# A low-rank-adapted matrix product: W on the sync queue, other load pieces, warm-up transpositions, no early store

## The chip, the cores and the metric

The kernel runs on one core of a Trainium2 chip. The metric is the device time of one execution in microseconds (us); lower is better. The profiled span, from the first to the last instruction of the program, is about 1.3 us shorter than that time.

## The reference

```python
x: (16, 2048, 256) float32      # 32768 rows of 256
W: (256, 256); lora_A: (256, 16); lora_B: (16, 256); lora_E: (16,); scale = 1.0

y = x_flat @ W
lora_out = ((x_flat @ lora_A) * lora_E) @ lora_B
return (y + scale * lora_out).reshape(16, 2048, 256)
```

x is 33.6 MB and y is 33.6 MB, and each has to cross between HBM and the on-chip memory once. The kernel folds the low-rank part into the weight, `weff = W + scale * A·diag(E)·B`, and does one product of x with `weff` in bf16.

## The kernel before

x is cut into eight chunks of 4 MB (128 partitions, 32 rows of 256 floats in each). Six "homes" hold a chunk each; the result overwrites x in its home, and chunks 6 and 7 take the homes of chunks 0 and 1 once these have been stored. Every chunk is worked on in eight groups of four rows. A group goes from POOL (cast to bf16) to PE (transposition), ACT (copy out of PSUM, the memory that PE writes to), PE (product) and DVE (copy back into the home). The sync engine issues all the x loads and y stores; their order is a list. All small operands come through the scalar engine's queue.

```python
LOAD_PIECES = {0: [8, 8, 16]}          # chunk 0 is loaded in three pieces
ORDER = ["L0", "L1", "L2", "L3", "L4", "L5",
         "S0", "S1", "L6", "L7", "S2", "S3", "S4", "S5", "S6", "S7"]
EARLY_AFTER = 1
...
def load(pc):                          # sync engine
    c, s, e = pc
    if c == N_HOMES - 1:
        sync.wait_ge(s_weff, 1)        # W, A, B lie in the last home until weff is made
    if c >= N_HOMES:
        sync.wait_ge(stored_of[c - N_HOMES], 16)
    ...
for step in ORDER:
    if step[0] == "L":
        ...load the pieces of chunk c...
        if c == EARLY_AFTER:           # the early store: 16 partitions x 128 B of group 0
            sync.wait_ge(s_first, 1)   # DVE has finished group 0
            sync.dma_start(out=y_chunks[0, :16, 0, :32], in_=home(0)[:16, 0, :32]).then_inc(s_early, 16)
    else:
        sync.wait_ge(s_chunk, c + 1)
        if c == 0:
            sync.wait_ge(s_early, 16)
        sync.dma_start(out=y_chunks[c], in_=home(c)[:])...
...
# PE, after the set-up products and turn(0), turn(1):
for i in ...:                          # software pipeline, PE works in this order
    turn(i + 2)                        # four transpositions of group i + 2
    multiply(i)                        # eight products of group i
```

Of the kernel before, what the change touches and what calls it, by code (L numbers as in the profile page):

```python
# [7 lines left out]
P = 128  # L8
# [5 lines left out]
ROWS = 32  # L14
N_CHUNKS = 8
N_HOMES = 6
LOAD_PIECES = {0: [8, 8, 16]}

ORDER = [
    "L0", "L1", "L2", "L3", "L4", "L5",  # L20
    "S0", "S1", "L6", "L7", "S2", "S3", "S4", "S5", "S6", "S7",
]

EARLY_AFTER = 1

HELD = N_HOMES - 1

CG = 4
# [9 lines left out]
def kernel(  # L38
# [16 lines left out]
    KT = K // P  # L55
# [3 lines left out]
    y_chunks = out_flat.rearrange("(c p b) m -> c p b m", p=P, b=ROWS)  # L59

    sbuf, psum, sem = nc.alloc_sbuf_tensor, nc.alloc_psum_tensor, tc.alloc_semaphore
# [3 lines left out]
    ident = sbuf("ident", [P, P], FP32)  # L65

    last_home = homes[N_HOMES - 1]
    w_sb = last_home[:, 0:KT, :]
# [6 lines left out]
    psum_y = [psum(f"psum_y{i}", [P, CG, M], FP32) for i in range(NY)]  # L75

    pieces = []
    for c in range(N_CHUNKS):
        s = 0
        for n in LOAD_PIECES.get(c, [ROWS]):  # L80
            pieces.append((c, s, s + n))
            s += n
    loaded = {pc: sem(f"loaded_{pc[0]}_{pc[1]}") for pc in pieces}
    set_up_loaded = {n: sem(f"loaded_{n}") for n in ("w", "a", "b", "e")}
# [9 lines left out]
    s_y = sem("multiplied")  # L94
    s_free = sem("y_free")
    s_chunk = sem("chunk_done")
    s_first = sem("first_done")
    s_early = sem("early_stored")

    def home(c):  # L100
        return homes[c % N_HOMES]

    sync, gpsimd, scalar, vector, tensor = nc.sync, nc.gpsimd, nc.scalar, nc.vector, nc.tensor
# [20 lines left out]
    def sync_program():  # L124
        def load(pc):
            c, s, e = pc
            if c == N_HOMES - 1:
                sync.wait_ge(s_weff, 1)
            if c >= N_HOMES:
                sync.wait_ge(stored_of[c - N_HOMES], 16)  # L130
            ins = sync.dma_start(out=home(c)[:, s:e, :], in_=x_chunks[c, :, s:e, :])
            return ins.then_inc(loaded[pc], 16)

        opening.append(load(pieces[0]).ins.name)
        for step in ORDER:
            c = int(step[1:])
            if step[0] == "L":
                for pc in pieces:
                    if pc[0] == c and pc != pieces[0]:
                        load(pc)  # L140
                if c == EARLY_AFTER:

                    sync.wait_ge(s_first, 1)
                    sync.dma_start(out=y_chunks[0, :16, 0, :32], in_=home(0)[:16, 0, :32]).then_inc(s_early, 16)
            else:
                sync.wait_ge(s_chunk, c + 1)
                if c == 0:
                    sync.wait_ge(s_early, 16)
                sync.dma_start(out=y_chunks[c], in_=home(c)[:]).then_inc(stored_of.get(c, stored_rest), 16)

    def gpsimd_program():
# [26 lines left out]
    def scalar_program():  # L178
        for name, to, of in (
            ("a", a_sb, lora_A.rearrange("(q t) r -> q t r", t=KT)),  # L180
            ("e", e_sb[:], lora_E[:, None]),
            ("b", b_sb, lora_B),
            ("w", w_sb, W.rearrange("(q t) m -> q t m", t=KT)),
        ):
            ins = scalar.dma_start(out=to, in_=of).then_inc(set_up_loaded[name], 16)
            if name == "a":
                opening.append(ins.ins.name)
        for g in range(N_GROUPS):
            scalar.wait_ge(s_turned, g + 1)
            if g >= NX:  # L190
                scalar.wait_ge(s_y, g - NX + 1)
            halves = psum_xt[g % NT][:].bitcast(BF16).rearrange("q b (p t) -> q b t p", t=KT)
            scalar.copy(out=xt[g % NX][:], in_=halves).then_inc(s_xt, 1)  # L193

    def vector_program():
        vector.wait_ge(set_up_loaded["e"], 16)
        vector.wait_ge(s_pe_set_up, 1)
        vector.tensor_scalar(  # L198
            out=ate,
            in0=psum_y[0][:R, :KT, :P],  # L200
            scalar1=e_sb[:],
            scalar2=float(scale),
            op0=ALU.mult,
            op1=ALU.mult,
        ).then_inc(s_ate, 1)
        vector.wait_ge(set_up_loaded["w"], 16)
        vector.wait_ge(s_pe_set_up, 2)
        vector.tensor_add(out=weff[:], in0=w_sb, in1=psum_y[1][:, :KT, :]).then_inc(s_free, NY)  # L208
        vector.drain().then_inc(s_weff, 1)
        for g in range(N_GROUPS):  # L210
            c, b = g // GPC, g % GPC * CG
            vector.wait_ge(s_y, g + 1)
            vector.tensor_copy(out=home(c)[:, b:b + CG, :], in_=psum_y[g % NY][:]).then_inc(s_free, 1)  # L213
            if g == 0:
                vector.drain().then_inc(s_first, 1)
            if g % GPC == GPC - 1:
                vector.drain().then_inc(s_chunk, 1)

    def tensor_program():
        def take(s):  # L220
            tensor.wait_ge(s, 1).then_inc(s, -1)  # L221

        def turn(i):
            take(s_stage)

            words = stage[i % NS][:].bitcast(FP32)
            for b in range(CG):
                ins = tensor.transpose(psum_xt[i % NT][:, b, :], words[:, b, :], ident[:])  # L228
            ins.then_inc(s_turned, 1)

        def multiply(i):
            take(s_xt)
            take(s_free)
            for b in range(CG):
                for t in range(KT):
                    ins = tensor.matmul(  # L236
                        psum_y[i % NY][:, b, :],
                        xt[i % NX][:, b, t, :],
                        weff[:, t, :],
                        start=(t == 0),  # L240
                        stop=(t == KT - 1),
                    )
            ins.then_inc(s_y, 1)

        tensor.wait_ge(s_ident, 2)
        tensor.wait_ge(set_up_loaded["a"], 16)
        for t in range(KT):
            ins = tensor.transpose(psum_y[0][:R, t, :P], a_sb[:, t, :], ident[:])  # L248
        ins.then_inc(s_pe_set_up, 1)
        turn(0)  # L250
        tensor.wait_ge(set_up_loaded["b"], 16)
        tensor.wait_ge(s_ate, 1)
        for t in range(KT):
            ins = tensor.matmul(psum_y[1][:, t, :], ate[:, t, :], b_sb, start=True, stop=True)  # L254
        ins.then_inc(s_pe_set_up, 1)
        turn(1)
        assert N_GROUPS % UNROLL == 0 and all(UNROLL % n == 0 for n in (NS, NX, NT, NY))
        with tensor.Fori(0, N_GROUPS // UNROLL):
            for i in range(UNROLL):
                turn(i + 2)  # L260
                multiply(i)
# [6 lines left out]
    with tc.tile_critical(no_gpsimd_drain=True):  # L268
        sync_program()
        gpsimd_program()  # L270
        scalar_program()
        vector_program()
        tensor_program()
# [35 lines left out]
```

## Time and profile before

The median was 161.84 us in three runs (161.71 to 161.97).

| reading | before | view |
|---|---|---|
| span | 160.5 us | page, head |
| bytes moved, mean rate | 67.43 MB, 420 GB/s | page, DMA packets |
| sync engine's queue, share of the 16 DMA engines | 97.9% | page, DMA queues |
| PE, DVE busy | 59%, 50% | page, busy times |
| first x load issued, store 0 issued | 0.00, 28.16 us | timeline of the sync engine |
| last instruction of a compute engine ends | 122.0 us | chain that ended last |

The page of the kernel before: busy times of two engines, then the busy share of the 16 DMA engines in 40 slices of the span (in tenths, 9 is 90% or more), and the two queues with packets, MB and share of the engines' time (q1 is the sync engine's, q10 the scalar engine's).

```profile
span 160.5 us, 2160 instructions
...
PE 94.2 (59%) x782; PEld 83.9 (52%) x782; DVE 79.5 (50%) x66; ACT 66.0 (41%) x65; POOL 67.0 (42%) x70
...
DMA  7999999999999999999999999999999999999993
...
q1 hardware_dynamic: 2624, 67.11, 97.9%
q10 hardware_dynamic: 352, 0.30, 0.5%
```

No compute engine is near full; the transfer engines are full in every slice but the first and the last. The Trainium skill, "HBM Reference", section "Specifications (TRN2)", says that a core that streams alone reaches about 425 GB/s; the 420 GB/s over the whole span here, start and end included, agree with it.

The timeline of the sync engine before (start, length from the first to the last of a merged row, engine and line of the kernel, operation; "q" marks an engine's instruction queue). It shows when transfers enter the queue, not when their data move.

```profile
0.00 2.44 SPq L131 DMA_DIRECT2D home<-in_x_dram  x4
16.99 0.36 SPq L144 DMA_DIRECT2D out_dram<-home  x1
17.40 1.84 SPq L131 DMA_DIRECT2D home<-in_x_dram  x4
28.16 10.82 SPq L149 DMA_DIRECT2D out_dram<-home  x2
72.43 10.03 SPq L131 DMA_DIRECT2D home<-in_x_dram  x2
82.51 39.88 SPq L149 DMA_DIRECT2D out_dram<-home  x6
```

Chunks 0 and 1 (8.4 MB) are in the queue by 2.4 us. At 429 GB/s they last some 20 us from the first data at 1 us, so, with the small operands between them, until about 22 us (in the trace load 1 has landed at 22.8). The early store holds up loads 2 to 5 until 17.4 us, more than four us before the queue would run dry.

The waits of the kernel before (who waited for what: total us, times, longest), two that the change is aimed at:

```profile
POOL stage L173 <- DMA home<-in_x_dram: 7.5, 4, 3.0
...
DVE weff L208 <- DMA home<-in_W_dram: 5.9, 1, 5.9
```

and one from the sync engine's own list of waits:

```profile
SPq L144 <- DVEq L215: 14.5, 1, 14.5
```

The first row is POOL waiting for pieces of x, the second the merge of the weight waiting for W, the third the early store waiting for group 0.

The timeline of PE before, its first operations.

```profile
6.02 1.09 PE L228 MATMUL psum_xt<-ident,stage 128*128 128x128 f32 x4 [0.32 <-PEq L221]
...
9.34 1.97 PE L228 MATMUL psum_xt<-ident,stage 128*128 128x128 f32 x8
13.79 1.86 PE L236 MATMUL psum_y<-weff,xt 128*128 128x256 bf16 x8 [2.48 <-PEq L221]
```

The first product runs at 13.79 us, after the merge at 12.95 us, so W sets the start of the main loop.

### The profile page before, as it was taken

Reading aid. Unit: us, or ns where it says so; the run is one execution under the profiler, and the core shown is the slowest. Engines: PE = TensorE matmul, PEld = TensorE weight load, DVE = VectorE, ACT = ScalarE, POOL = GpSimd, SP = SyncE. Lnnn points to the kernel's source line nnn. Section 1 sums busy time; section 2 is a strip of 40 time slices with the busy share of each in tenths; the row PEclk is TensorE's granted clock in tenths of the full one; section 3 lists DMA queues with packets and bytes.
Section 4 is the critical chain, followed back from the end, with each engine's and each line's share of the span. In section 5 each row is a group of like instructions: output and inputs, shape, how many; then the busy total and the mean of one; then the engine's idle time right before and its main releaser. Section 6 shows DMA issues by size and latency. Waiting matters only on the chain. (4 is left out here: it accounts for less than half of the span.)

```text
span 160.5 us, 2160 instructions
## 1 busy us (share of the span) xinstructions
PE 94.2 (59%) x782; PEld 83.9 (52%) x782; DVE 79.5 (50%) x66; ACT 66.0 (41%) x65; POOL 67.0 (42%) x70
## 2 busy tenths in 40 slices
PE   0585979999999999400019999999990000000000
PEld 0354869999999999300017999899990000000000
DVE  0102796999999999700003799899993000000000
ACT  3240667777777777400005577777740000000000
POOL 1542648777777777000045577777700000000000
PEclk9999999999999999955555999999998555555555
DMA  7999999999999999999999999999999999999993
GB/s 262 432 425 466 449 393 425 490 392 408 498 400 392 492 400 400 400 417 466 425 400 451 457 392 433 474 402 425 466 400 433 466 408 433 449 425 417 441 449 155
DMA packets 2979, 67.43 MB, mean 420 GB/s; under 512 B 528, under 2 KB 544, under 8 KB 672
## 3 DMA queue, kind: packets, MB, share of 16 engines
q1 hardware_dynamic: 2624, 67.11, 97.9%
q10 hardware_dynamic: 352, 0.30, 0.5%
q14 instruction: 3, 0.02, 0.0%
HBM read 33.85 MB, written 33.56 MB: 420 GB/s over the span
## 5 line engine op out<-in xcount | busy, mean ns | idle before, releaser
L213 DVE COPY home<-psum_y 128x1024 f32<-128x1024 f32 x64 | 78.3, 1225 | 30.0 <-PE psum_y L236 25.3
L173 POOL CAST stage<-home 128x1024 bf16<-128x1024 f32 x64 | 66.3, 1040 | 47.5 <-PE psum_xt L228 21.4
L193 ACT COPY xt<-psum_xt 128x1024 bf16<-128x1024 bf16 x64 | 64.7, 1012 | 49.8 <-PE psum_xt L228 49.8
L236 PE MATMUL psum_y<-weff,xt 128*128 128x256 bf16 x512 | 69.4, 281 | 2.6 <-PEq L221 2.5
L236 PEld LDWEIGHTS psum_y<-weff,xt 128*128 128x128 bf16 x512 | 51.4, 101 | 9.6 <-issue 3.2
L228 PE MATMUL psum_xt<-ident,stage 128*128 128x128 f32 x264 | 42.5, 287 | 18.6 <-PEq L221 18.6
L228 PEld LDWEIGHTS psum_xt<-ident,stage 128*128 128x128 f32 x264 | 33.1, 149 | 21.1 <-issue 20.2
L198 DVE TENSOR_SCALAR home<-psum_y,e_sb 16x256 f32<-16x256 f32 x1 | 0.5, 472 | 6.6 <-DMA e_sb<-in_lora_E_dram 6.6
L208 DVE TENSOR_TENSOR weff<-home,psum_y 128x512 bf16<-128x512 f32 x1 | 0.7, 689 | 5.9 <-DMA home<-in_W_dram 5.9
L248 PE MATMUL psum_y<-ident,home 128*16 128x128 f32 x2 | 0.6, 394 | 5.1 <-DMA home<-in_lora_A_dram 5.1
L248 PEld LDWEIGHTS psum_y<-ident,home 128*16 128x16 f32 x2 | 0.1, 87 | 5.1 <-issue 5.1
L193 ACT ACT_TABLE_LOAD x1 | 1.3, 1283 | 2.5 <-issue 2.5
L254 PE MATMUL psum_y<-home 16*128 16x256 f32 x4 | 2.1, 670 | 0.2 <-DMA home<-in_lora_B_dram 0.2
L254 PEld LDWEIGHTS psum_y<-home 16*128 16x128 f32 x4 | 1.2, 319 | 0.8 <-DMA home<-in_lora_B_dram 0.6
L152 POOL MEMSET ident<- 128x128 f32 x1 | 0.2, 204 | 0.7 <-SPq L268 0.7
L154 POOL TENSOR_SCALAR_AFFINE_SELECT ident<-ident 128x128 f32<-128x128 f32 x1 | 0.3, 292 | 0.2 <-POOL ident L152 0.2
L290 POOL MEMSET const-float32-0.0<- 128x1 f32 x1 | 0.1, 98 | 0.2 <-issue 0.2
L290 POOL MEMSET const-bfloat16-1.0<- 128x1 bf16 x1 | 0.1, 101 | 0.0
L290 POOL MEMSET const-uint8-127<- 128x1 uint8 x1 | 0.1, 101 | 0.0
L290 POOL MEMSET const-float32-1.0<- 128x1 f32 x1 | 0.1, 98 | 0.0
## 6 DMA issues: line engine op xcount, KB each, us to landing
out_dram<-home SPq DMA_DIRECT2D x8, 4096.0 KB, 39.7
home<-in_x_dram SPq DMA_DIRECT2D x7, 4096.0 KB, 20.8
home<-in_x_dram SPq DMA_DIRECT2D x2, 1024.0 KB, 5.7
home<-in_x_dram SPq DMA_DIRECT2D x1, 2048.0 KB, 11.5
home<-in_W_dram ACTq DMA_DIRECT2D x1, 256.0 KB, 10.9
home<-in_lora_A_dram ACTq DMA_DIRECT2D x1, 16.0 KB, 4.9
e_sb<-in_lora_E_dram ACTq DMA_DIRECT2D x1, 0.1 KB, 5.5
home<-in_lora_B_dram ACTq DMA_DIRECT2D x1, 16.0 KB, 5.8
```

The source lines that it names most:

```text
L152: gpsimd.memset(ident[:], 0.0).then_inc(s_ident, 1)
L154: gpsimd.affine_select(out=ident[:], in_=ident[:], compare_op=ALU.not_equal, fill=1.0, base=0, pattern=[[-1, P]], channel_multiplier=1,).t ...
L173: gpsimd.tensor_copy(out=stage[g % NS][:], in_=home(c)[:, b:b + CG, :]).then_inc(s_stage, 1)
L193: scalar.copy(out=xt[g % NX][:], in_=halves).then_inc(s_xt, 1)
L198: vector.tensor_scalar(out=ate, in0=psum_y[0][:R, :KT, :P], scalar1=e_sb[:], scalar2=float(scale), op0=ALU.mult, op1=ALU.mult,).then_inc(s ...
L208: vector.tensor_add(out=weff[:], in0=w_sb, in1=psum_y[1][:, :KT, :]).then_inc(s_free, NY)
L213: vector.tensor_copy(out=home(c)[:, b:b + CG, :], in_=psum_y[g % NY][:]).then_inc(s_free, 1)
L228: ins = tensor.transpose(psum_xt[i % NT][:, b, :], words[:, b, :], ident[:])
L236: ins = tensor.matmul(psum_y[i % NY][:, b, :], xt[i % NX][:, b, t, :], weff[:, t, :], start=(t == 0), stop=(t == KT - 1),)
L248: ins = tensor.transpose(psum_y[0][:R, t, :P], a_sb[:, t, :], ident[:])
L254: ins = tensor.matmul(psum_y[1][:, t, :], ate[:, t, :], b_sb, start=True, stop=True)
L290: nc = _bacc.Bacc("TRN2", target_bir_lowering=False, num_devices=1)
```

## The change

The intent is an earlier start: W arrives right behind the first eight rows of x, PE is warm when real work comes, chunk 1 can be started when half of it is there, and nothing makes the sync engine wait before loads 2 to 5.

```diff
-LOAD_PIECES = {0: [8, 8, 16]}
+LOAD_PIECES = {0: [8, 24], 1: [16, 16]}
+WARM_UP = 12
-EARLY_AFTER = 1
 ...
         opening.append(load(pieces[0]).ins.name)
+        sync.dma_start(out=w_sb, in_=W.rearrange("(q t) m -> q t m", t=KT)).then_inc(set_up_loaded["w"], 16)
         for step in ORDER:
 ...
-                if c == EARLY_AFTER:
-                    sync.wait_ge(s_first, 1)
-                    sync.dma_start(out=y_chunks[0, :16, 0, :32], in_=home(0)[:16, 0, :32]).then_inc(s_early, 16)
             else:
                 sync.wait_ge(s_chunk, c + 1)
-                if c == 0:
-                    sync.wait_ge(s_early, 16)
 ...                                              # scalar engine's loads
-            ("w", w_sb, W.rearrange("(q t) m -> q t m", t=KT)),
 ...                                              # DVE
-            if g == 0:
-                vector.drain().then_inc(s_first, 1)
 ...                                              # PE
         tensor.wait_ge(s_ident, 2)
+        for i in range(WARM_UP):
+            tensor.transpose(psum_y[1][:, i % CG, :P], ident[:], ident[:])
         tensor.wait_ge(set_up_loaded["a"], 16)
```

More of the change, by code (lines that the diff above doesn't have):

```diff
@@ L96 @@
     s_chunk = sem("chunk_done")
-    s_first = sem("first_done")
-    s_early = sem("early_stored")
     def home(c):
```

## The prediction

> **What bounds the kernel now.** The page gives a span of 160.5 us, and the DMA row of the 40 slices shows 9 tenths or more in every slice but the first (7) and the last (3). 67.43 MB move at a mean of 420 GB/s; the sync engine's queue alone takes 97.9% of the 16 DMA engines' time, the scalar engine's 0.5%. In two-us windows the DMA share is 0.50 from 0 to 2 us, averages about 1.0 from 2 to 158, and falls to 0.08 at 158 to 160: start-up, gapless transfers, stragglers. The compute engines have slack: PE is 59% busy, DVE 50%; the waits show POOL idle 18.6 us in one piece for stores to free a buffer, and the chain that ended last stops at 122 us, 38 us before the end; after it come only queued stores. The Trainium skill, "DMA: Bandwidth & Descriptors", section "Issuing engines are not separate DMA queues", says that DMAs of all issuing engines run on the same 16 DMA engines and interleave. The trace agrees: the two queues' shares add up to one full set of engines.
>
> **What the change does.**
> - W (256 KB) goes from the scalar to the sync queue. Its bytes cost about 0.6 us at 420 GB/s on either. Before, it was issued at 1.99 us and landed 10.9 us later; the weight merge on DVE waited 5.9 us for it and ran at 12.95. Now it follows 1 MB of x and should land near 6. The merge then waits for the B product on PE (7.34 to 9.41) and runs near 10: 3 us earlier.
> - With chunk 0 in pieces of 8 and 24 rows the second piece lands near 12.5 us; groups 0 and 1 multiply before, group 2 near 14.5. Chunk 1 in halves removes POOL's wait of 2.11 us at 22.8. Compute of the first five chunks ends near 64 instead of 67.4 us.
> - Twelve warm-ups, about 0.27 us each by the early transpositions (4 in 1.09 us), fill PE from 1.9 to 5.2 us, just when A lands (5.1): no harm.
> - Dropping the early store removes sync's 14.5 us wait, so loads 2 to 4 are issued near 4 us, load 5 near 10, instead of 17.4 to 19.2. But the queue never drained before: loads 0 and 1 kept it busy until about 22. The store itself is 2 KB: nothing.
>
> **On the critical path.** Almost none of it. The same bytes go through the same queue in nearly the same order, with no gap to close. Store 0 is issued near 24 instead of 28.16 us, but its data moves only after load 5, near 60. Loads 6 and 7 still wait for stores 0 and 1 (issued at 72.4 and about 82), which the queue's order fixes. I expect -0.3 to +0.5 us; the plus is for the first large store, should the tiny early store have made it cheaper (the load-to-store turn at 58 to 61 us is the only risky stretch).
>
> **Time: 161.9 us, 8 in 10 between 161.0 and 162.7.** Faster by over 2%: 2%; within 2%: 96%; slower by over 2%: 2%.
>
> **What would show it.** W lands near 6 us and the merge runs near 10; the wait for the early store is gone; loads 2 to 5 issue before 11; store 0 issues near 24; yet the DMA row stays at 9 throughout, near 420 GB/s, load 6 is issued near 72, and the last store's data ends within 1 us of before.
>
> **What would make it wrong.** Gaps or longer transfers in the DMA row near 60 us, if a first store without the tiny one is slow; a lower DMA rate with 20 MB queued at once; one DMA engine finishing late.

## More of the kernel before

The windows of the kernel before. Each row has the window and its length in us, then the busy us (and the count of instructions) of PE, PE's weight loads, DVE, ACT and POOL. The last three columns are the granted PE clock, the DMA engines' busy share, and the GB/s of the transfers that started in the window.

```profile
2.00:28.00 26.00, 18.95 (x123) 15.14 (x124) 10.88 (x10) 12.01 (x12) 12.98 (x13) 1.00 1.01 429
...
56.00:64.00 8.00, 8.00 (x76) 7.44 (x75) 7.49 (x7) 6.10 (x7) 6.24 (x6) 1.00 1.02 406
64.00:158.00 94.00, 39.23 (x332) 35.19 (x329) 34.97 (x29) 26.29 (x26) 24.91 (x24) 0.71 1.00 432
158.00:162.00 4.00, 0.00 (x0) 0.00 (x0) 0.00 (x0) 0.00 (x0) 0.00 (x0) 0.50 0.04 16
```

Over long windows the rate is the same whether loads or stores run. A window of eight us is a coarse measure, because a transfer counts whole in the window where it starts: between 28 and 56 us, where loads alone move, such windows of this kernel read from 397 to 459 GB/s. So the 406 at 56 to 64 us, where the queue turns from load 5 to store 0, shows no dip by itself.

## The result

The changed kernel took 161.93 us (median of 4 runs, 161.73 to 162.15), the kernel before 161.78 us beside it (4 runs, 161.56 to 161.97). The ratio is 1.001, with a 95% interval of 0.9989 to 1.0031. Ratios here and below are the mean time of one kernel's fast runs over the mean of the other's fast runs of the same rounds, so they are not quite the ratio of the medians quoted. Executions over 1.5% slower than the fastest of the same kernel are left out of the means.

The page of the changed kernel.

```profile
span 160.8 us, 2180 instructions
...
PE 94.7 (59%) x794; PEld 85.0 (53%) x794; DVE 79.5 (49%) x66; ACT 66.1 (41%) x65; POOL 67.1 (42%) x70
...
DMA  7999999999999999999999999999999999999993
...
q1 hardware_dynamic: 2736, 67.37, 98.0%
q10 hardware_dynamic: 208, 0.03, 0.1%
```

The DMA row is the same digit for digit. W's 0.26 MB have moved from one queue to the other, and the sum of the shares has stayed at 98%.

The windows of the changed kernel, the same stretches.

```profile
2.00:28.00 26.00, 19.18 (x124) 15.63 (x125) 9.73 (x9) 11.22 (x11) 12.14 (x12) 0.80 1.01 425
...
56.00:64.00 8.00, 8.00 (x76) 7.43 (x74) 7.49 (x7) 6.21 (x7) 6.38 (x7) 1.00 1.04 431
64.00:158.00 94.00, 39.49 (x343) 35.80 (x340) 36.14 (x30) 27.16 (x27) 25.81 (x25) 0.74 1.00 431
158.00:162.00 4.00, 0.00 (x0) 0.00 (x0) 0.00 (x0) 0.00 (x0) 0.00 (x0) 0.50 0.06 25
```

The rates are equal within 1% but for the turn at 56 to 64 us, 431 against 406 GB/s, which the scatter of such short windows covers. The single transfers, which the kept traces hold one by one, show a smaller difference: with the bytes of each spread over its own duration, 424 against 415 GB/s moved from 56 to 72 us, some 0.3 us, in one profile of each kernel. The total did not get shorter by it: transfers still start in the last window (25 against 16 GB/s), and the first 26 us ran at 425 against 429. The lower granted clock of PE in the first window (0.80; it is 0.50 from 10 to 19 us) belongs to the stretch where PE waits for x.

The timeline of the sync engine after.

```profile
0.00 0.38 SPq L128 DMA_DIRECT2D home<-in_x_dram  x1
1.14 0.33 SPq L132 DMA_DIRECT2D home<-in_W_dram  x1
1.52 9.67 SPq L128 DMA_DIRECT2D home<-in_x_dram  x7
29.33 10.82 SPq L141 DMA_DIRECT2D out_dram<-home  x2
72.73 10.03 SPq L128 DMA_DIRECT2D home<-in_x_dram  x2
82.81 38.85 SPq L141 DMA_DIRECT2D out_dram<-home  x6
```

All loads up to load 5 are in the queue by 11.2 us instead of 19.2. But load 6 enters at 72.73 against 72.43 us: it waits for store 0 to land, and that is set by the bytes ahead of it.

The waits of the changed kernel, the same subjects.

```profile
POOL stage L165 <- DMA home<-in_x_dram: 10.2, 2, 6.8
...
DVE weff L199 <- PE psum_y L245: 3.6, 1, 3.6
```

The early store's wait is gone, and the merge no longer waits for W but for the product with B. POOL, however, now waits 6.8 us in one piece for the 24 rows of chunk 0.

The timeline of PE after.

```profile
6.38 0.63 PE L217 MATMUL psum_xt<-ident,stage 128*128 128x128 f32 x4 [0.43 <-PEq L210]
...
9.89 1.11 PE L217 MATMUL psum_xt<-ident,stage 128*128 128x128 f32 x4
15.24 1.08 PE L217 MATMUL psum_xt<-ident,stage 128*128 128x128 f32 x4 [4.23 <-PEq L210]
16.11 1.91 PE L225 MATMUL psum_y<-weff,xt 128*128 128x256 bf16 x8
```

The first product runs at 16.11 us, 2.3 us later than before, although the merge ran at 10.10 instead of 12.95 us. The row above it tells why: the transpositions of group 2 stand before the product of group 0 in PE's program, and group 2 belongs to the 24-row piece, which POOL got at 14.05 us.

So the change made the start of the main loop later, not earlier, and that cost nothing. Two explanations stand against each other.

- **Theory.** The transfer queue is full from 1 to 158 us in both kernels; nothing that the change does lies on that path, in either direction, as long as the queue does not run dry.
- **Rival.** The parts have effects of half a us to one us that cancel: for example W early gains, the missing early store loses, or the late start of the main loop hides a gain.

### The profile page after: what moved, and what is told of

It is laid out like the page before. It is cut to its first block, busy times and chain, and to the rows that moved or that the text cites. A ratio compares the mean times of both kernels' runs of the same rounds, so it can differ in the third digit from the quotient of the medians.

```text
span 160.8 us, 2180 instructions
## 1 busy us (share of the span) xinstructions
PE 94.7 (59%) x794; PEld 85.0 (53%) x794; DVE 79.5 (49%) x66; ACT 66.1 (41%) x65; POOL 67.1 (42%) x70
## 5 line engine op out<-in xcount | busy, mean ns | idle before, releaser
L217 PE MATMUL psum_xt<-ident,stage 128*128 128x128 f32 x264 | 42.0, 284 | 21.2 <-PEq L210 21.2
L217 PEld LDWEIGHTS psum_xt<-ident,stage 128*128 128x128 f32 x264 | 32.4, 147 | 23.7 <-issue 22.9
L236 PE MATMUL psum_y<-ident 128*128 128x128 f32 x12 | 2.8, 426 | 1.9 <-POOL ident L146 1.9
L236 PEld LDWEIGHTS psum_y<-ident 128*128 128x128 f32 x12 | 2.4, 227 | 1.9 <-POOL ident L146 1.9
L245 PE MATMUL psum_y<-home 16*128 16x256 f32 x4 | 1.4, 479 | 1.6 <-DMA home<-in_lora_B_dram 1.6
L245 PEld LDWEIGHTS psum_y<-home 16*128 16x128 f32 x4 | 0.7, 184 | 1.9 <-DMA home<-in_lora_B_dram 1.8
## 6 DMA issues: line engine op xcount, KB each, us to landing
home<-in_x_dram SPq DMA_DIRECT2D x1, 3072.0 KB, 12.5
```

What stands on the lines that cost most here:

```text
L217: ins = tensor.transpose(psum_xt[i % NT][:, b, :], words[:, b, :], ident[:])
L236: tensor.transpose(psum_y[1][:, i % CG, :P], ident[:], ident[:])
L245: ins = tensor.matmul(psum_y[1][:, t, :], ate[:, t, :], b_sb, start=True, stop=True)
```

## The experiments

Each kernel was run beside the kernel before on the same chip; "before" below is the median of those runs. Results were correct in all runs but one. The warm-ups were not run alone; experiment 10 against the changed kernel bounds what they and the early W do together (ratios to the kernel before of 1.0005 and 1.001).

### 1. One part alone: no early store

```diff
-                if c == EARLY_AFTER:
-                    sync.wait_ge(s_first, 1)
-                    sync.dma_start(out=y_chunks[0, :16, 0, :32], in_=home(0)[:16, 0, :32]).then_inc(s_early, 16)
...
-                if c == 0:
-                    sync.wait_ge(s_early, 16)
...
-            if g == 0:
-                vector.drain().then_inc(s_first, 1)
```

> Edit: the kernel before without the early store and its two waits; nothing else. Theory (the transfer queue is full from 1 to 158 us, so no part of the change is on the path): 161.8 us, within 0.3 of before; loads 2 to 5 issue near 3 to 14 us instead of 17.4; the load-to-store turn at 58 to 61 us keeps its stretched 32 KB transfers of 1.5 to 1.7 us, no more of them. Rival (parts cancel: the early store had made the first large store cheap, and W and the warm-ups pay for its loss): 0.5 to 1.5 us slower than before, with longer transfers near 60 us.

Measured: 162.03 us (6 runs), before 162.24 (11 runs, 10 of them fast), ratio 0.9985 (0.9951 to 1.0018). The turn at 56 to 64 us ran at 427 GB/s, and of the transfers that started from 56 to 66 us 7 took over 1.5 us, against 22 in the kernel before (one profile of each). So a first large store without the tiny one ahead of it is not slower; the rival falls for this part.

### 2. One part alone: W on the sync queue

```diff
+        sync.dma_start(out=w_sb, in_=W.rearrange(...)).then_inc(set_up_loaded["w"], 16)
-            ("w", w_sb, W.rearrange("(q t) m -> q t m", t=KT)),
```

> Edit: the kernel before with W loaded through the sync queue behind the first eight rows of x; early store, pieces and no warm-ups as before. Theory: within 0.3 us of before (161.8); the merge on DVE near 10 us instead of 12.95, group 0 multiplied near 11 to 12 instead of 13.8, early store issued near 14 to 15 instead of 17. Rival (parts cancel): 0.5 to 1.5 us faster than before.

Measured: 161.84 us (6 runs), ratio 0.9987 (0.9955 to 1.0019). The merge ran at 9.20 us and the early store went out at 14.00 us, so the earlier start is real, three us of it, and no part of it reaches the end.

### 3. One part alone: the pieces

```diff
-LOAD_PIECES = {0: [8, 8, 16]}
+LOAD_PIECES = {0: [8, 24], 1: [16, 16]}
```

> Edit: the kernel before with chunk 0 in pieces of 8 and 24 rows and chunk 1 in halves. Theory: group 0 is multiplied only after group 2 has been turned, so the 24-row piece sets the first multiplication near 15 to 16 us; the early store goes out near 18.5 to 19.5, still ahead of the queue's draining at 22; total within 0.3 us of before (161.8). Rival (parts cancel): the pieces alone cost 0.5 to 1 us.

Measured: 164.09 us (6 runs, one of them slow), ratio of the fast runs 1.0083 (1.0029 to 1.0136). This is a miss: the early store went out at 20.33 us, a little later than expected, and the time grew by over one us. Experiments 9 to 11 follow it up. The sync engine's timeline of this run, the early store and the four loads after it:

```profile
20.33 0.36 SPq L144 DMA_DIRECT2D out_dram<-home  x1
20.74 1.85 SPq L131 DMA_DIRECT2D home<-in_x_dram  x4
```

### 4. The changed kernel with three pieces for chunk 0

```diff
-LOAD_PIECES = {0: [8, 24], 1: [16, 16]}
+LOAD_PIECES = {0: [8, 8, 16], 1: [16, 16]}
```

> Edit: the changed kernel with chunk 0 in three pieces (8, 8, 16) as before, chunk 1 in halves. Theory: the 24-row piece was what held the first multiplication (PE runs turn 2 before multiply 0), so now it runs near 11 us instead of 16.1, store 0 issues near 24 to 25 us instead of 29.3, and the time stays at 161.8, within 0.3 us of the kernel before. Rival (the changed kernel would gain were it not for its late compute): 0.5 to 1.5 us faster than before.

Measured: 161.97 us (6 runs), ratio 0.9996 (0.9964 to 1.0029). The timeline of PE of this run:

```profile
9.16 1.97 PE L217 MATMUL psum_xt<-ident,stage 128*128 128x128 f32 x8
10.92 1.91 PE L225 MATMUL psum_y<-weff,xt 128*128 128x256 bf16 x8
```

and of its sync engine:

```profile
24.17 15.94 SPq L141 DMA_DIRECT2D out_dram<-home  x2
```

Group 2 is turned together with group 1, the first product runs at 10.92 instead of 16.11 us, and store 0 is issued at 24.17 instead of 29.33 us. So the 24-row piece was what held the main loop up in the changed kernel. And five us of an earlier start of compute gain nothing. (Compute does not end earlier: PE then waits 3.6 us for chunk 2, whose load landed at 33.05 us.)

### 5 and 6. Compute later, by 160 and by 480 transpositions

```diff
         turn(1)
+        for i in range(160):     # 480 in the second kernel
+            tensor.transpose(psum_xt[3][:, i % CG, :], ident[:], ident[:])
```

> Edit: the changed kernel with 160 extra transpositions on PE after group 1 has been turned (some 17 us of PE at 0.11 us each). Theory (compute has slack until the queue drains near 60 us): the first multiplication moves from 16 to about 28 to 30 us, store 0 from 29.3 to 41 to 43, the time stays at 161.9, within 0.4. Rival (compute timing matters, a part of its delay shows): at least 2 us slower.

> Edit: as the last, with 480 extra transpositions (some 52 us). Theory: store 0 issues near 77 us, past the point near 60 where the loads end, so the queue stands empty for 16 to 19 us and the time is 178 to 182 us. It shows where the slack ends. Rival (store 0 was not what the queue needed next): under 170 us.

Measured: with 160, 163.59 us (4 runs, 163.26 to 163.96), before 162.38, ratio 1.0083 (1.0037 to 1.013). Store 0 was issued at 41.87 us, 12.5 us later than in the changed kernel. The spans were 161.2 to 161.4 us against 160.4 to 161.4 of the kernel before, so little of the extra time (a mean of 0.3 us) lies inside the span: the times exceed the spans by 2.1 to 2.6 us here, against 1.3 us in the other kernels. The expectation of 161.9 ± 0.4 was missed; experiment 12 repeats this with another program.

With 480, 180.09 us (2 runs). Store 0 was issued at 75.49 us. Of the page of this run, the DMA row:

```profile
DMA  7999999999999600098899999899989999999994
```

The queue stands empty between about 61 and 76 us (three slices of 0), after load 5 and before store 0. Store 0 came 46.2 us later than in the changed kernel and the time grew by 18.2 us, so about 28 us of the delay were free. (The two kernels were not run beside each other; against the kernel before of the same rounds, 162.38 us, the growth is 17.7 us, which leaves 28.5 us.) This fits the place where the loads end: 29.3 + 28 gives 57, and the last load's data end near 61.

### 7. The same wait, where the queue is short

```diff
-EARLY_AFTER = 1
+EARLY_AFTER = 0
```

> Edit: the kernel before with its early store one step earlier in the sync queue, behind chunk 0's loads instead of chunk 1's. The same wait for group 0, but with only 4 MB queued ahead of it. Theory: chunk 0's data ends near 12 us, the wait ends near 17, the next data start about 1 us after that: a gap of 5 to 6 us, and 167 to 168.5 us in all. Rival (a wait of the sync engine costs nothing here): 161.8.

Measured: 168.50 us (2 runs), before 162.38, ratio 1.0381. The page and the sync engine's timeline of this run:

```profile
DMA  7990799999999999999999999999999999999994
```

```profile
0.00 1.94 SPq L131 DMA_DIRECT2D home<-in_x_dram  x3
16.89 0.36 SPq L144 DMA_DIRECT2D out_dram<-home  x1
```

The wait ended at 16.89 us, as in the kernel before (16.99); but only chunk 0 was queued ahead of it, and the fourth slice of the row is 0. The wait is the same and its price goes from nothing to over six us. What it costs is the time for which the queue is empty after it.

### 8. Fewer bytes

```diff
-                sync.dma_start(out=y_chunks[c], in_=home(c)[:])...
+                n = ROWS // 2 if c == N_CHUNKS - 1 else ROWS
+                sync.dma_start(out=y_chunks[c, :, :n], in_=home(c)[:, :n, :])...
```

> Edit: the changed kernel storing only 16 of the 32 rows of the last chunk, 2.1 MB less (wrong result on purpose: the rest of the output is never written). Theory (bytes set the time): 2.1 MB at 427 GB/s are 4.9 us, so 157.0 us, within 0.5. Rival (something else sets the end): less than 2 us gained.

Measured: 156.86 us (2 runs), wrong result. That is 5.1 us less than the changed kernel, which was measured in other rounds, and 5.5 us less than the kernel before of the same rounds (162.38 us): 2.1 MB less at 380 to 413 GB/s, not far from the mean rate of 420. So bytes move the time at about the queue's rate; that compute does not until the queue runs dry rests on experiments 4, 6 and 12.

### 9 and 10. The pieces again, with and without the early store

Experiment 9 is the kernel of experiment 3 unchanged; experiment 10 is both edits, that of 1 and that of 3:

```diff
-LOAD_PIECES = {0: [8, 8, 16]}
+LOAD_PIECES = {0: [8, 24], 1: [16, 16]}
-                if c == EARLY_AFTER:
-                    ...the early store, its wait and its signals...
```

> The kernel of the run pieces once more, for a comparison on one chip with the next. That run missed its expectation: the wait for the early store ended at 20.33 us, 2 us ahead of the draining of the queue at 22.4, and the first transfers of load 2 took up to 2.0 us instead of 1.21. New theory (a load issued less than about 2 us ahead of draining meets a cold start, as the kernel's first load does): 163 to 164.7 us again, with stretched transfers at 22 to 28 us. Rival (that run was a slow state): 161.9 us.

> Edit: the run pieces without the early store and its two waits. Theory (the pieces cost time only through the early store's wait): 161.9 us, within 0.3 of the kernel before, no stretched transfers between 20 and 28 us. Rival (the 24-row and 16-row pieces cost time themselves): 163 us or more.

Measured: the pieces again 163.71 us (6 fast runs, 162.79 to 164.47), before 162.25 (11 runs, 161.71 to 162.99), ratio 1.0102 (1.0065 to 1.014). The pieces without the early store 162.34 us (6 runs), ratio 1.0005 (0.9973 to 1.0037). So the loss is real, and the pieces cause it only together with the early store.

The 12 runs of the pieces with the early store (experiments 3 and 9) lie in two groups, 162.3 to 163.2 us (5 runs) and 164.1 to 164.8 us (7 runs). The profile of the run pieces (span 163.4 us, the one run counted as slow) is of the upper group, that of pieces_again (161.5 us, a fast one) of the lower. The windows from 2 to 28 us of these two, and then of pieces_no_early (161.3 us):

```profile
2.00:28.00 26.00, 16.75 (x94) 12.81 (x95) 7.92 (x8) 9.58 (x10) 10.46 (x11) 1.00 0.99 401
```

```profile
2.00:28.00 26.00, 16.69 (x91) 12.73 (x92) 7.61 (x8) 9.38 (x9) 10.29 (x10) 1.00 1.02 425
```

```profile
2.00:28.00 26.00, 16.34 (x93) 12.54 (x94) 7.81 (x8) 9.47 (x10) 10.35 (x11) 1.00 1.01 424
```

These rows show a loss in the first alone, but the single transfers, which the kept traces hold one by one, show it in both runs with the early store. Of the 32 KB transfers that started between 20 and 28 us, 21 in pieces and 12 in pieces_again took over 1.5 us, up to 2.04 and 2.21 us instead of the usual 1.21; in pieces_no_early none took longer than 1.21. With the bytes of each transfer spread over its own duration, 363 and 400 GB/s moved from 20 to 28 us with the early store and 433 without it, worth 1.3 and 0.6 us. So a cold start of load 2, issued only about 1.6 us ahead of the draining at 22.4 us, is a part of the loss, and it stands in the fast run too.

The rest is not settled. Near the turn, from 56 to 66 us, transfers of over 1.5 us stand in every run: 15 in pieces, 31 in pieces_again, 10 in pieces_no_early, 22 in the kernel before. The last store sums up what was lost: the first of the 16 transfer engines was done with it at 159.8 and 159.4 us in the two runs, against 158.3 us in pieces_no_early and 158.5 us in the kernel before. The span ends with the last engine, which was 2.0 to 3.6 us behind the first in these four profiles, and that spread differs from run to run: the span of pieces_again is only 0.2 us longer than that of pieces_no_early, though its first engine was 1.0 us later.

### 11. The changed kernel with the early store put back

```diff
+                if c == EARLY_AFTER:
+                    sync.wait_ge(s_first, 1)
+                    sync.dma_start(out=y_chunks[0, :16, 0, :32], in_=home(0)[:16, 0, :32]).then_inc(s_early, 16)
...
+                if c == 0:
+                    sync.wait_ge(s_early, 16)
...
+            if g == 0:
+                vector.drain().then_inc(s_first, 1)
```

> Edit: the changed kernel with the early store and its two waits put back. Theory: group 0 leaves DVE at 19.3 us (18.07 and 1.22 in the changed kernel), so the early store is issued near 19.4 and load 2 near 19.8, 2.5 us ahead of the draining near 22.4: 161.9 to 162.8 us, some of the cold start at 22 to 28 us but less than in pieces. Rival (the early store itself costs or gains nothing whenever it comes): 161.9 within 0.2. Rival (parts cancel, the early store gains): below 161.5.

Measured: 161.96 us (6 runs, 161.67 to 162.75), ratio 0.9991 (0.9963 to 1.0019). The early store went out at 18.91 us and load 2 at 19.31, about 3 us ahead of the draining, and the turn ran at 435 GB/s. Only one transfer of load 2 took over 1.5 us, and the first transfer engine was done with the last store at 158.4 us. So with W early (and the warm-ups) the wait ends soon enough even with the 24-row piece, and the early store neither costs nor gains. Compare the loads' issue in experiment 3 at 20.74 us: 1.4 us later it costs 1%.

### 12. The delay of experiment 5 as a hardware loop

```diff
         turn(1)
+        with tensor.Fori(0, 40):
+            for i in range(4):
+                tensor.transpose(psum_xt[3][:, i % CG, :], ident[:], ident[:])
```

> Edit: late_a with its 160 transpositions as a hardware loop of 40 times 4 instead of 160 instructions. In late_a the spans were 161.2 to 161.4 us, at the upper end of those of before, but the times 2.1 to 2.6 us above the spans, against 1.3 elsewhere. Theory (delay of compute is free; the excess came with the longer program, outside the span): first multiplication near 28 to 30 us as in late_a, span 160.4 to 161.2, time 161.8 to 162.4. Rival (the delay costs 1 us): 163.2 us or more.

Measured: 162.64 us (6 runs, 162.15 to 162.95), before 162.25, ratio 1.0028 (1.0003 to 1.0054), spans 160.8 to 161.6 us. Store 0 was issued at 42.38 us. The times are again 1.3 us above the spans, so the larger excess of experiment 5 did not come from the delay of compute. Which feature of that program made it is not settled: the kernel with 480 transpositions in a row, longer still, had an excess of 1.3 us. The time is 0.2 us above the range that I had given; 13 us of delay went with a median 0.4 us higher, and the times alone cannot tell how much of that is the spread of the kernel before, whose 11 runs reach from 161.71 to 162.99 us, though the interval just excludes 1. The traces help: the first of the 16 transfer engines was done with the last store at 158.3 us here and 158.4 us in experiment 5, against 158.5 us in the kernel before and 158.3 us in the changed one. So the delay of compute did not push the queue back; what was later is the last engine (161.2 us in both, against 160.4 and 160.8), in one profile of each. The rival figure of 163.2 us or more is excluded.

No run pointed to a version that beats both kernels by more than the noise; the fastest median of a new complete one was 161.84 us (experiment 2).

## Why the prediction was right, and where it was not

- **"The same bytes go through the same queue in nearly the same order, with no gap to close."** Right. The DMA row is identical, the marginal MB costs about what the rate says (experiment 8), and a start of compute earlier by 5 us (4) or later by 13 us (12), or W earlier by 3 us (2), moves the time by at most 0.3%. Predicted 161.9, measured 161.93 us.
- **"W lands near 6 us and the merge runs near 10."** Right. W was issued at 1.14 us and landed 4.7 us later; the merge ran at 10.10 us.
- **"Loads 2 to 5 issue before 11."** Right but for 0.2 us: the row of issues ends at 11.19 us. Load 6 was issued at 72.73 us, as predicted near 72.
- **"Groups 0 and 1 multiply before, group 2 near 14.5", and so "store 0 issues near 24" and compute "ends near 64 instead of 67.4 us".** Wrong. Group 0 was multiplied at 16.11 us, and store 0 was issued at 29.33 us. The step that failed is the order on PE: `turn(i + 2)` stands before `multiply(i)`, so group 0 waits for group 2 to be turned, and group 2 was in the large piece. That piece was also mis-sized: available to POOL at 14.05 us instead of 12.5. With the piece cut in two the predicted 24 us came out (24.17, experiment 4). The failed step did not touch the time, because store 0 has some 28 us of slack (experiment 6). The end of compute failed for another reason too. DVE's copies before its long pause ended at 20.17 + 48.38 = 68.55 us, and in experiment 4, with the early start, still at 68.51: there PE, ahead of the loads, waited for chunk 2 (landed at 33.05 us), and the 24 copies that followed took 31.4 us. Nor is that the end of five chunks, as the 67.4 us was read in the prediction: it is 38 copies of 40, since the last two groups of chunk 4 stand in PE's program behind groups of chunk 5, which POOL could cast only at 82.6 us, when stores 0 and 1 had freed buffers.
- **"Twelve warm-ups ... no harm."** Right. They ended at 4.75 us, and PE then waited another 0.6 us for A. They bought little: the next four transpositions took 0.63 instead of 1.09 us, but those at 9.89 and 15.24 us took 1.11 and 1.08 us again. In experiment 4, with the same warm-ups, even the next four took 1.09 us.
- **"The plus is for the first large store, should the tiny early store have made it cheaper."** It had not: 0.9985 without it (1), and the turn was no slower than with it.
- **"Dropping the early store ... nothing."** Right for this change as a whole, too simple as a reason, and so in part luck. I judged the parts one by one and missed that two of them interact: with W late, the new pieces push the early store's wait to 20.3 us, and that costs 1.0% (experiments 3 and 9). Either other part of the change, no early store (10) or W early (11), removes the cost. So the early store was a wait with four to five us of margin in the kernel before, and the changed kernel has no such wait at all.

## What to carry to other kernels

When the transfer queue is full from end to end, ask of each change one thing: can the queue run dry, and how far ahead of that moment is the next transfer issued? The same wait cost nothing with four to five us of queue left, about 1% with 1.6 us left, and over 6 us with the queue empty. And when a load is cut into pieces for an in-order, software-pipelined engine, cut it at the group that the engine needs before its first product, not at the group which that product consumes.

## What the Trainium skill lacked or had wrong

- "TensorE: Matmul & The Clock Gate", section "Part 4: PE-mode transpose", says that the full clock does not engage for transpositions. Here it did, for fp32 transpositions: in experiment 6 PE ran nothing but transpositions from 10.15 to 63.5 us. The granted clock was 0.50 in the window from 11 to 12 us, with 7 transpositions in it, and 1.00 from 13 to 14 us, with 12; from 20 to 60 us it stayed at 1.00, with some 186 in 20 us (0.108 us each).
- "DMA: Bandwidth & Descriptors", section "Where 436 GB/s comes from", says that for transfers between HBM and the on-chip memory the HBM side (about 358 GB/s per core) binds. With one core running, 425 to 433 GB/s were measured in the long windows through loads and stores alike, which the page "HBM Reference" has right; the section itself calls a measured 425 GB/s near the fabric's rate.
- No page that I read says what a transfer queue loses when it is refilled just ahead of running dry: with load 2 issued some 1.6 us ahead the kernel lost 0.8 to 1.0% (experiments 3 and 9), with about 3 us ahead nothing (experiment 11).
- No page that I read has the slow turn from loads to stores. With the bytes of each transfer spread over its own duration, 401 to 428 GB/s moved from 56 to 72 us in the 12 kernels and runs whose queue stayed full, against 430 to 433 from 28 to 56 us, and single 32 KB transfers there took up to 2.5 us instead of 1.21. The cause is open.
- No page that I read gives a size for the drift between the 16 transfer engines on a full queue: on the last store the last of them was done 2.0 to 3.6 us after the first in the four profiles of experiments 9 and 10 and the kernel before, and that ends the span.
